# First and last RMS norms of an encoder layer: weight row spread by TensorE, roots by ScalarE and VectorE, last token tile in two halves of its columns

## The chip, the cores and the metric

The kernel runs on one core of a Trainium2 chip. The metric is the device time of one execution in microseconds (us); a kernel's time is the median of its runs. TensorE multiplies matrices, VectorE, ScalarE and GpSimd work elementwise, SyncE issues most of the transfers (DMA); each engine runs its own instructions in the order in which they were compiled and waits for the others by semaphores.

## The reference

One layer of a bidirectional encoder over 1024 tokens of width 1024, all in float32, with 256 memory tokens. Each of three parts is normed ahead and behind and added to the residual stream:

```python
def _rms_norm(x, gain):
    xf = x.astype(jnp.float32)
    y = xf * lax.rsqrt(jnp.mean(xf * xf, axis=-1, keepdims=True) + EPS)
    return (y * gain.astype(jnp.float32)).astype(x.dtype)
...
h = _rms_norm(x, g_mix_pre[l])
proj = h @ w_in[l]
...   # window attention and gated DeltaNet on the columns of proj
x = x + _rms_norm(mix, g_mix_post[l])
...   # cross-attention into the memory
x = x + _rms_norm(c, g_cross_post[l])
f = _swiglu(_rms_norm(x, g_ffn_pre[l]), w_gate_up[l], w_down[l])
x = x + _rms_norm(f, g_ffn_post[l])
```

The change concerns the first of these norms (with `g_mix_pre`, EPS is 1e-6) and the last (with `g_ffn_post`) with the product by `w_down` ahead of it (2816 rows, 1024 columns).

## The kernel before

**Numbers.** TensorE takes a float32 operand as a pair: `split` (L100) has ScalarE round the source to the array's short form (`hi`, the cast in L103) and VectorE or GpSimd subtract it from the source (`lo`, L104). A product is three matmuls, hi by hi, hi by lo, lo by hi, which add up in one PSUM bank of 128 x 512 float32. "Plain" float32 products, with operands that are not split, occur too; the transposes by the identity (`ident`) are of this kind.

**Order.** The program is written with a tile framework. Pools hand out tiles in on-chip memory (SBUF, 128 partitions); a pool stacks its tiles from the low end of memory or, with `side="right"`, from the high end, each tile rounded up to 32 bytes a partition. Tiles of one pool with the same `tag` share `bufs` buffers, so the next one waits until the earlier one has been read. At compile time a scheduler orders each engine's instructions against a timeline of its own; `tc.high_priority(AHEAD)` draws the block's instructions forward in it, and `tc.issue_after(ins)` puts the block's instructions behind `ins` on the engine they share. So the order of the text is not the order of an engine: a change in one place can move instructions elsewhere.

**Memory.** Pool `cst` (L112) holds `ident`, `mhalf` (a constant -0.5) and `cols` at the low end; all pools of the left side, with the weight pool `wp` (L117) first, lie above it. On the right side a filler tile of 32 bytes (`off`, L115) lies ahead of the others.

**The start (L202 to L233).** Six of eight token tiles `xt` (128 tokens x 1024) are loaded at once on SyncE's queue; behind the first come `gmix`, the row `g_mix_pre` repeated for all 128 partitions by the transfer (512 KB), and `ident`. For each tile t: ScalarE squares it into a scrap tile `junk` and sums (`ss`, L221), `rstd_of` (L158) makes the inverse root by two GpSimd instructions (scale and add EPS, L161; power -0.5, L162), VectorE multiplies tile, root and `gmix` (L224), TensorE transposes eight 128 x 128 pieces into two PSUM tiles (L229), and `split` makes `hi` and `lo` of them. Four tiles fill one half (`hT[0]`: `hhi0`, `hlo0`), four the other. Two weight blocks of `w_in` are loaded behind the second and fourth tile (`load_w` in the line of `ws`, `after=xload[t]`) and multiplied by the halves as these get ready (`gemm_b`, L261). What is read from other parameters meanwhile: two mask copies `mU_r`, `mL_r` (L247, L248) on VectorE, three small loads into `prm` (L250 to L252), `nega`, an exponential on ScalarE (L253), and the narrow weight tile `wabr` (L307) on VectorE.

**The middle** (DeltaNet, attention, output projection, cross-attention, gate and up products) is not touched.

**The last product and the end (L1635 to L1768).** The product by `w_down` is made of seven block products of half the tokens by half the columns (11 blocks of 128 rows each); `block_product` makes them for four token tiles at once, into the banks `A`, `D_` and `X` of 128 x 512. The seventh is written out in the loop at L1744: for each of four token tiles t, two strips of the left operand (`atr`, 6 and 5 blocks) are loaded and split, and 33 matmuls add to `X[t]`, which already holds the product before it. The sums that are not `X`'s lie in `za` (columns 512 to 1023 of the output, finished before) and `zv` (columns 0 to 511). Then VectorE adds the bank (L1761), `sq_of` (L1674) has ScalarE square and sum 512 columns into `sq`, VectorE multiplies by the gain row `gp` (which holds the gain times the root of 1024, so that the norm needs a sum and not a mean), `rstd_at` (L1688) makes the root on GpSimd from both halves' sums, and VectorE finishes `za` and `zv` with the root and the residual (`residual`, L1682, loaded again from `d_x2`) and SyncE stores each:

```python
    nc.vector.tensor_tensor(zv[:, t], zv[:, t], X[t], ALU.add)
    sq_of(zv[:, t], r, 0)
    nc.vector.tensor_tensor(zv[:, t], zv[:, t], gp[:, 0:512], ALU.mult)
    rs = rstd_at(r)
    for z, o_ in ((za, 512), (zv, 0)):
        nc.vector.scalar_tensor_tensor(z[:, t], z[:, t], rs, xr[:, o_:o_ + 512], ALU.mult, ALU.add)
        nc.sync.dma_start(out[there(r), o_:o_ + 512], z[:, t])
```

`first_half` (L1723) finishes the other four token tiles, two of them inside this loop. `bank` (L1500) takes a PSUM bank from a pool of eight; four are free by then.

Of the kernel before, what the change touches and what calls it, by code (L numbers as in the profile page):

```python
# [10 lines left out]
F32 = mybir.dt.float32  # L11
F32R = mybir.dt.float32r
I32 = mybir.dt.int32
AF = mybir.ActivationFunctionType
ALU = mybir.AluOpType
# [4 lines left out]
P = 128  # L20
S = 1024
D = 1024
# [4 lines left out]
EPS = 1e-6  # L27
# [49 lines left out]
def tile_hybrid_block(  # L77
# [4 lines left out]
    g_ffn_pre, w_gate_up, w_down, g_ffn_post, consts, out, dump=None, stop=None,  # L82
):
    nc = tc.nc
    x, mem, out = x[0], mem[0], out[0]
# [26 lines left out]
    cst = ctx.enter_context(pool("cst", 1))  # L112
# [20 lines left out]
    ident = cst.tile([P, P], F32, name="ident")  # L133
    mhalf = cst.tile([P, 16], F32, name="mhalf")
    nc.gpsimd.memset(mhalf, -0.5)
    cols = cst.tile([P, P], F32, name="cols")
    p12 = ExitStack()
    sm = p12.enter_context(pool("sm", 1))
# [2 lines left out]
    mU_r = sm.tile([P, P], F32R, name="mU_r")  # L141
    mL_r = sm.tile([P, P], F32R, name="mL_r")
    prm = sm.tile([P, 24], F32, name="prm")
    nega = sm.tile([P, 8], F32, name="nega")
# [10 lines left out]
    cm = {n: (C[:, a - C0:a - C0 + P] if a < C1 else CE[:, a - C1:a - C1 + P]) for n, a in _AT.items() if n != "ident"}  # L155
    rope_f, rope_s = (CE[:, _ROPE_AT - C1 + i:_ROPE_AT - C1 + i + 1] for i in range(2))

    def rstd_of(rs, ss, n, eps):  # L158

        w = ss.shape[-1]  # L160
        nc.gpsimd.tensor_scalar(rs, ss, n, eps, ALU.mult, ALU.add)  # L161
        nc.gpsimd.tensor_tensor(rs, rs, mhalf[:, :w], ALU.pow)  # L162


    gain_at = {"cross": 60, "mem": 60 + KT, "ffn": 60 + 2 * KT}
    r0 = 60 + 3 * KT
# [29 lines left out]
    t1 = pa1.enter_context(pool("t1a", 2, side="right"))  # L196

    def small():
        return ps.tile([P, 512], F32, tag="ps", name="ps")


    xts = [t1.tile([P, D], F32, tag="xt", name="xt", bufs=6) for _ in range(6)]  # L202
    gmix = t1.tile([P, D], F32, tag="gmix", name="gmix", bufs=1)
    xload = []
    for t in range(6):
        xload.append(nc.sync.dma_start(xts[t], x[t * P:(t + 1) * P, :]))
        if t == 0:
            nc.sync.dma_start(gmix, g_mix_pre[0].partition_broadcast(P))
            nc.sync.dma_start(ident, consts[:, 0:P])
    hT = []  # L210
    for hf in range(2):
        hi = hx.tile([P, KT, HALF], F32R, name=f"hhi{hf}")
        lo = hx.tile([P, KT, HALF], F32R, name=f"hlo{hf}")
        for j in range(4):
            t = 4 * hf + j
            xt = xts[t] if t < 6 else t1.tile([P, D], F32, tag="xt", name="xt", bufs=6)
            if t >= 6:
                nc.sync.dma_start(xt, x[t * P:(t + 1) * P, :])
            junk = t1.tile([P, D], F32, tag="junk", name="junk", bufs=1)
            ss = t1.tile([P, 1], F32, tag="ss", name="ss", bufs=4)  # L220
            nc.scalar.activation(junk, xt, AF.Square, accum_out=ss)  # L221
            rs = t1.tile([P, 1], F32, tag="rs", name="rs", bufs=4)
            rstd_of(rs, ss, 1.0 / D, EPS)
            nc.vector.scalar_tensor_tensor(xt, xt, rs, gmix, ALU.mult, ALU.mult)  # L224
            for kq in range(2):
                pt = small()
                for k in range(4):
                    c = (4 * kq + k) * P
                    nc.tensor.transpose(pt[:, k * P:(k + 1) * P], xt[:, c:c + P], ident)  # L229
                o = slice(4 * kq, 4 * kq + 4), slice(j * P, (j + 1) * P)  # L230
                split(hi[:, o[0], o[1]], lo[:, o[0], o[1]], pt.rearrange("p (k t) -> p k t", k=4))
        hT.append((hi, lo))
        dump(f"hT{hf}", (hi, lo))  # L233
# [8 lines left out]
    pt = small()  # L242
# [1 line left out]
    nc.scalar.copy(cols, pt[:, :P])  # L244
    nc.sync.dma_start(CE, consts[:, C1:])
    nc.sync.dma_start(C, consts[:, C0:C1])
    nc.vector.tensor_copy(mU_r, cm["mU"])  # L247
    nc.vector.tensor_copy(mL_r, cm["mL"])  # L248

    nc.sync.dma_start(prm[:, 0:8], a_log[0].rearrange("d h -> (d h)").partition_broadcast(P))  # L250
    nc.sync.dma_start(prm[:, 8:16], dt_bias[0].rearrange("d h -> (d h)").partition_broadcast(P))
    nc.sync.dma_start(prm[:, 16:24], attn_sink[0].partition_broadcast(P))  # L252
    nc.scalar.activation(nega, prm[:, 0:8], AF.Exp)  # L253
    nc.vector.tensor_scalar(nega, nega, -1.0, None, ALU.mult)

    def gemm_b(whi, wlo, act, psums, nk=KT):
# [45 lines left out]
    t1 = pa1.enter_context(pool("t1b", 1, side="right"))  # L302
# [1 line left out]
    wab = t1.tile([P, KT, 16], F32, tag="wab", name="wab", bufs=1)  # L304
    nc.sync.dma_start(wab, w_in[:, 2816:2832].rearrange("(k p) n -> p k n", p=P))
    wabr = tb.tile([P, KT, P], F32R, tag="V", name="wabr", bufs=1)
    nc.vector.tensor_scalar(wabr, hT[0][0].bitcast(F32)[:, :, 0:P], 0.0, None, ALU.mult)  # L307
    nc.vector.tensor_copy(wabr[:, :, 0:16], wab)
    nc.vector.tensor_tensor(wabr[:, :, 16:32], wab, f32(wabr[:, :, 0:16]), ALU.subtract)
    abT = tb.tile([32, S], F32, tag="A", name="abT", bufs=1)  # L310
    for hf in range(2):
        pp = pg.tile([P, 512], F32, tag="pg", name="pg")
        for k in range(KT):
            for a in range(2):
                nc.tensor.matmul(pp, wabr[:, k, :], hT[hf][a][:, k, :], start=(k == 0 and a == 0),
                                 stop=(k == KT - 1 and a == 1))
        nc.scalar.copy(abT[:, hf * HALF:(hf + 1) * HALF], pp[0:32, :])
    pt = small()
# [1180 lines left out]
    def bank(name):  # L1499
        return pg.tile([P, 512], F32, tag="pg", name=name)  # L1500
# [172 lines left out]

    def sq_of(src, t, ch):  # L1674
        jk = tp_.tile([P, 512], F32, tag="jk", name="jk", bufs=1)
        nc.scalar.activation(jk, src, AF.Square, accum_out=sq[:, ch, t:t + 1])  # L1676

    def there(t):
        r = (t + NT // 2) % NT
        return slice(r * P, (r + 1) * P)  # L1680
# [7 lines left out]
    def rstd_at(t):  # L1688

        rs = tp_.tile([P, 1], F32, tag="frs", name="frs")  # L1690
        nc.gpsimd.tensor_scalar(rs, sq[:, 1, t:t + 1], sq[:, 0, t:t + 1], D * EPS, ALU.add, ALU.add)  # L1691
        nc.gpsimd.tensor_tensor(rs, rs, mhalf[:, 0:1], ALU.pow)
        return rs
# [46 lines left out]
    for t in range(4):  # L1740
        nc.vector.tensor_tensor(za[:, t], za[:, t], X[t], ALU.add)
        sq_of(za[:, t], 4 + t, 1)

    for t in range(4):  # L1744
        tt = slice(t * P, (t + 1) * P)
        for k0, n in ((0, 6), (6, 5)):
            with tc.high_priority(AHEAD):
                ar = wp.tile([P, KT, P], F32, tag="wraw", name="atr")[:, 0:n]
                nc.sync.dma_start(ar, d_a["22"][k0:k0 + n, :, tt].rearrange("f p n -> p f n"))
                ah, al = [wp.tile([P, KT, P], F32R, tag=g, name=g)[:, 0:n] for g in ("whi", "wlo")]  # L1750
                split(ah, al, ar)
            for k in range(n):
                for i, (a, w) in enumerate(((ah, t4h), (ah, t4l), (al, t4h))):
                    nc.tensor.matmul(X[t], a[:, k], w[:, k0 + k], start=False, stop=(k0 + k == NB - 1 and i == 2),  # L1754
                                     skip_group_check=True)
        if t < 2:
            first_half(2 + t)
        r = 4 + t
        xr = residual(r)
        nc.vector.tensor_tensor(za[:, t], za[:, t], gp[:, 512:], ALU.mult)  # L1760
        nc.vector.tensor_tensor(zv[:, t], zv[:, t], X[t], ALU.add)  # L1761
        sq_of(zv[:, t], r, 0)
        nc.vector.tensor_tensor(zv[:, t], zv[:, t], gp[:, 0:512], ALU.mult)
        rs = rstd_at(r)
        for z, o_ in ((za, 512), (zv, 0)):
            nc.vector.scalar_tensor_tensor(z[:, t], z[:, t], rs, xr[:, o_:o_ + 512], ALU.mult, ALU.add)
            nc.sync.dma_start(out[there(r), o_:o_ + 512], z[:, t])
    LB.close()  # L1768
    L0.close()

# [29 lines left out]
```

## Time and profile before

| | us |
|---|---|
| median of three runs | 1534.2 |
| lowest and highest | 1531.57, 1537.82 |
| the profiled execution | 1537.92 |
| its span, from first to last instruction or transfer | 1536.2 |
| TensorE busy, 0 to 30 / 30 to 1500 / 1500 to 1528.3 / behind it | 16.89 / 1431.81 / 28.28 / 0.00 |

The profiled execution ran at a granted TensorE clock of 0.992 (1 is full speed). In the profile, an operation is named by engine and line: PE is a matmul on TensorE, PEld the load of its stationary operand, DVE VectorE, ACT ScalarE, POOL GpSimd, SP SyncE; a "q" behind it is the engine's sequencer, which waits and issues. `ps<-ident,xt` is a tile and what it is made from; `x16` counts the instructions that a row takes together; what stands in brackets is the idle time ahead of it and what ended it. A matmul's own duration overlaps with the next one's, so a row of n matmuls is read by its whole length. In a window's row each engine has its busy time and number of instructions, in the order PE, PEld, DVE, ACT, POOL; then the granted clock and the transfers. In a row of a group, the numbers behind the bar are busy us of all, mean ns of one, and idle us of the engine ahead of them.

### The profile page before, as it was taken

To read this page: it belongs to the slowest core of one execution; us is meant where nothing else is said; L and a number is where in the kernel's file an instruction comes from. 1 tells how busy PE (TensorE), PEld (TensorE's weight loads), DVE (VectorE), ACT (ScalarE), POOL (GpSimd) and SP (SyncE) were. 2 spreads that over 40 slices of the span, in tenths; PEclk is the share of its full clock that TensorE was granted. 3 is DMA by queue.
4 is the path that set the end of the run, shared out by engine and by line. 5 is a ranking of instruction groups with operands and counts; after the bars stand their busy time and mean duration, and the time that the engine had idled before them with its cause. 6 is when DMAs were issued, how large, how long until landed. Compare 5 with 4: busy or idle time off the path is not lost.

```text
span 1536.2 us, 21190 instructions
## 1 busy us (share of the span) xinstructions
PE 1477.0 (96%) x7403; PEld 1241.1 (81%) x7403; DVE 1109.5 (72%) x1790; ACT 742.3 (48%) x1516; POOL 396.3 (26%) x404
## 2 busy tenths in 40 slices
PE   6999999999999999999999898999999999999997
PEld 5888878878899778887888686888888888888786
DVE  6868999787888865538466876676877555696665
ACT  5678821447557764456454663323223332454532
POOL 2020221311326203242201622343443332000021
PEclk9999999999999999999999999999999999999999
DMA  6235575856987684457725534343533333863354
GB/s 207 76 105 151 144 194 152 218 161 181 317 285 233 196 284 155 152 160 261 236 89 185 192 129 125 124 131 110 172 123 102 104 103 103 317 214 95 106 176 166
DMA packets 272360, 258.70 MB, mean 168 GB/s; under 512 B 34793, under 2 KB 204670, under 8 KB 272254
## 3 DMA queue, kind: packets, MB, share of 16 engines
q1 hardware_dynamic: 272253, 257.35, 53.3%
q8 instruction: 58, 0.95, 0.3%
q14 instruction: 49, 0.39, 0.1%
HBM read 179.41 MB, written 75.27 MB: 166 GB/s over the span
## 4 chain that ended last, share of the span: by engine, by line
PE 70%; DVE 11%; DMA 8%; ACT 6%; issue 3%; SPq 1%; POOL 1%; DVEq 0%; POOLq 0%; ACTq 0%
PE pE L1466 8%; PE pD L1466 8%; PE pA L1466 7%; PE pg L261 6%; PE pmg L1070 6%; PE pdX L1657 6%; PE pcq L261 4%; PE pdA L1657 4%; PE pB L1466 4%; PE pst L1286 3%; PE psc L809 2%; PE pdX L1754 2%; PE pdD L1657 2%; DVE acc L286 2%; DMA wraw<-in_w_ckv_dram 1%
## 5 line engine op out<-in xcount | busy, mean ns | idle before, releaser
L103 ACT CAST whi<-wraw 128x1024 fp32r<-128x1024 f32 x96 | 100.9, 1052 | 142.6 <-DMA wraw<-in_w_gate_up_dram 29.5
L104 POOL TENSOR_TENSOR wlo<-wraw,whi 128x1024 fp32r<-128x1024 f32 x38 | 91.9, 2419 | 188.9 <-ACT whi L103 180.2
L261 PE MATMUL pg<-hlo,whi 128*128 128x512 f32 x352 | 139.5, 397 | 0.0
L261 PE MATMUL pg<-hhi,whi 128*128 128x512 f32 x352 | 139.2, 396 | 0.0
L261 PE MATMUL pg<-hhi,wlo 128*128 128x512 f32 x352 | 138.4, 394 | 0.0
L1466 PE MATMUL pA<-b,whi 128*128 128x512 f32 x352 | 113.1, 402 | 5.9 <-ACT m L1483 3.4
L104 DVE TENSOR_TENSOR wlo<-wraw,whi 128x1024 fp32r<-128x1024 f32 x58 | 73.7, 1272 | 42.2 <-ACT whi L103 39.7
L1466 PEld LDWEIGHTS pA<-b,whi 128*128 128x128 f32 x352 | 67.4, 193 | 20.3 <-ACT m L1483 3.8
L1657 PE MATMUL pdX<-dhl,whi 128*128 128x512 f32 x264 | 76.1, 391 | 1.5 <-ACT dhl L103 0.8
L261 PEld LDWEIGHTS pg<-hhi,whi 128*128 128x128 f32 x352 | 66.5, 189 | 13.3 <-ACT hhi L103 0.2
L261 PEld LDWEIGHTS pg<-hhi,wlo 128*128 128x128 f32 x352 | 66.5, 189 | 12.8
L261 PEld LDWEIGHTS pg<-hlo,whi 128*128 128x128 f32 x352 | 66.4, 189 | 12.7
L1544 POOL TENSOR_TENSOR act<-act,up 128x512 f32<-128x512 f32 x33 | 49.5, 1501 | 95.9 <-DVE up L1543 62.6
L1466 PE MATMUL pA<-b,wlo 128*128 128x512 f32 x176 | 69.9, 398 | 0.0
L103 ACT CAST whi<-araw 128x1024 fp32r<-128x1024 f32 (+1 forms) x36 | 35.3, 981 | 67.7 <-PE pdX L1657 24.4
L104 DVE TENSOR_TENSOR wlo<-araw,whi 128x1024 fp32r<-128x1024 f32 (+1 forms) x36 | 40.8, 1134 | 35.0 <-ACT whi L103 34.9
L1516 POOL TENSOR_TENSOR sr<-wraw 128x512 f32<-128x512 f32 x22 | 30.0, 1366 | 130.4 <-DMA wraw<-in_w_gate_up_dram 119.1
L286 DVE SCALAR_TENSOR_TENSOR acc<-cp,cols,acc 128x1024 f32<-128x1024 f32 x48 | 62.1, 1295 | 0.1
L1691 POOL TENSOR_SCALAR frs<-sq 128x1 f32<-128x1 f32 x8 | 11.9, 1496 | 193.6 <-ACT jk L1676 192.7
L1657 PEld LDWEIGHTS pdX<-dhl,whi 128*128 128x128 f32 x264 | 49.3, 188 | 12.8 <-ACT dhl L103 1.1
L1466 PE MATMUL pB<-s0h,s1h 128*128 128x512 f32 x176 | 54.4, 391 | 3.4 <-ACT s1h L103 3.4
L103 ACT CAST dhl<-b 128x512 fp32r<-128x512 f32 x66 | 40.3, 620 | 31.6 <-PE pdA L1657 13.7
(481 smaller groups left out, 4302.2 us busy)
## 6 DMA issues: line engine op xcount, KB each, us to landing
wraw<-in_w_gate_up_dram SPq DMA_DIRECT2D x52, 512.0 KB, 3.9
kv<-d_kv SPq DMA_DIRECT2D x32, 512.0 KB, 6.8
wraw<-in_w_in_dram SPq DMA_DIRECT2D x22, 512.0 KB, 4.2
b<-in_w_down_dram SPq DMA_DIRECT2D x20, 512.0 KB, 7.7
araw<-d_as SPq DMA_DIRECT2D x20, 512.0 KB, 3.7
pz<-d_pz SPq DMA_DIRECT2D x32, 256.0 KB, 7.3
wraw<-in_w_ckv_dram SPq DMA_DIRECT2D x16, 512.0 KB, 5.1
wraw<-in_w_out_dram SPq DMA_DIRECT2D x16, 512.0 KB, 3.7
```

The source lines that it names most:

```text
L103: nc.scalar.copy(hi, src)
L104: (eng or nc.vector).tensor_tensor(lo, src, f32(hi), ALU.subtract)
L261: nc.tensor.matmul(p_, w[:, k, :], ah[a][:, k, :], start=(k == 0 and i == 0), stop=(k == nk - 1 and i == 2))
L286: nc.vector.scalar_tensor_tensor(acc, cp[:, t:t + S], taps[t], acc, ALU.mult, ALU.add)
L809: nc.tensor.matmul(out[:, d, h, :], lt[:, d, h, :], rt[:, d, h, :], start=True, stop=True)
L1070: nc.tensor.matmul(pp[t], act[a][:, k, tt], w_[:, kk, :], start=(k == 0 and i == 0), stop=(k == KT - 1 and i == 2))
L1286: nc.tensor.matmul(bank, a[:, tt], w, start=(start and i == 0), stop=(stop and i == 2), skip_group_check=not check)
L1466: nc.tensor.matmul(out_, w[a][:, k, :], xx[b_][:, k, :], start=(start and k == 0 and i == 0), stop=(k == HK - 1 and i == 2), skip_group_ch ...
L1516: nc.gpsimd.tensor_tensor(s[0], b_[:, 0:HK], b_[:, HK:], ALU.add)
L1544: nc.gpsimd.tensor_tensor(o_, o_, up, ALU.mult)
L1657: nc.tensor.matmul(banks[t], a[:, k - k0, tt], w, start=(first and k == 0 and i == 0), stop=(k == NB - 1 and i == 2), skip_group_check=not ...
L1754: nc.tensor.matmul(X[t], a[:, k], w[:, k0 + k], start=False, stop=(k0 + k == NB - 1 and i == 2), skip_group_check=True)
```

## The change

At the start, `gmix` is no longer spread by the transfer. A single row `grow` (4 KB) is loaded ahead of all, and two plain float32 matmuls against a row of ones, `one`, write it to 128 partitions of two PSUM tiles, from which VectorE copies it. `grow` has the tag of `junk`, which has one buffer. The inverse roots are ScalarE's square root (with scale, and EPS from a tile `epsc`) and VectorE's reciprocal (`inverse_root`) in place of two GpSimd instructions; a root of EPS (`warm`) is made ahead of them. `mU_r`, `mL_r` and `wabr` are ordered behind the last tile's scaling on VectorE and `nega` behind its root on ScalarE.

At the end, the fourth token tile's 33 matmuls of 512 columns become 33 of columns 0 to 255, into the bank it had, and 33 of columns 256 to 511, into a new bank `XL`, to which nothing was added before; the earlier content of that half of `X[3]` is added to `zv` ahead of the loop. Sum, square and gain are done for each half, `known` collects EPS and the sums on VectorE, the root is made by `inverse_root`, in all four tiles, and the fourth tile's `zv` is finished and stored in two halves. The strips' two inner loops become one list, `tiles`.

```diff
@@ constants
+    epsc = cst.tile([P, 1], F32, name="epsc")
+    nc.gpsimd.memset(epsc, EPS)
@@ behind rstd_of
+    def inverse_root(rs, ss, scale, bias):
+        root = nc.scalar.activation(rs, ss, AF.Sqrt, bias=bias, scale=scale)
+        nc.vector.reciprocal(rs, rs)
+        return root
@@ the start
+    grow = t1.tile([1, D], F32, tag="junk", name="grow", bufs=1)
+    one = cst.tile([1, P], F32, name="one")
+    nc.gpsimd.memset(one, 1.0)
     xload = []
     for t in range(6):
+        if t == 0:
+            nc.sync.dma_start(grow, g_mix_pre)
         xload.append(nc.sync.dma_start(xts[t], x[t * P:(t + 1) * P, :]))
         if t == 0:
-            nc.sync.dma_start(gmix, g_mix_pre[0].partition_broadcast(P))
             nc.sync.dma_start(ident, consts[:, 0:P])
+    warm = t1.tile([P, 1], F32, tag="ss", name="warm", bufs=4)
+    nc.scalar.activation(warm, epsc, AF.Sqrt)
+    for ch in range(2):
+        pt = small()
+        nc.tensor.matmul(pt, one, grow[:, ch * 512:(ch + 1) * 512], start=True, stop=True)
+        nc.vector.tensor_copy(gmix[:, ch * 512:(ch + 1) * 512], pt)
...
-            rstd_of(rs, ss, 1.0 / D, EPS)
-            nc.vector.scalar_tensor_tensor(xt, xt, rs, gmix, ALU.mult, ALU.mult)
+            rooted = inverse_root(rs, ss, 1.0 / D, epsc)
+            scaled = nc.vector.scalar_tensor_tensor(xt, xt, rs, gmix, ALU.mult, ALU.mult)
...
-    nc.vector.tensor_copy(mU_r, cm["mU"])
-    nc.vector.tensor_copy(mL_r, cm["mL"])
+    with tc.issue_after(scaled.ins):
+        nc.vector.tensor_copy(mU_r, cm["mU"])
+        nc.vector.tensor_copy(mL_r, cm["mL"])
...
-    nc.scalar.activation(nega, prm[:, 0:8], AF.Exp)
+    with tc.issue_after(rooted.ins):
+        nc.scalar.activation(nega, prm[:, 0:8], AF.Exp)
...
-    nc.vector.tensor_scalar(wabr, hT[0][0].bitcast(F32)[:, :, 0:P], 0.0, None, ALU.mult)
+    with tc.issue_after(scaled.ins):
+        nc.vector.tensor_scalar(wabr, hT[0][0].bitcast(F32)[:, :, 0:P], 0.0, None, ALU.mult)
@@ sq_of
-        nc.scalar.activation(jk, src, AF.Square, accum_out=sq[:, ch, t:t + 1])
+        nc.scalar.activation(jk[:, 0:src.shape[-1]], src, AF.Square, accum_out=sq[:, ch, t:t + 1])
@@ the end
+    nc.vector.tensor_tensor(zv[:, 3, 256:], zv[:, 3, 256:], X[3][:, 256:], ALU.add)
+    XL = bank("pdY")
 
     for t in range(4):
         tt = slice(t * P, (t + 1) * P)
+        tiles = []
...
-            for k in range(n):
+            tiles += [(ah[:, k], al[:, k]) for k in range(n)]
+        columns = [(slice(0, 512), X[t])] if t < 3 else [(slice(0, 256), X[t][:, 0:256]), (slice(256, 512), XL[:, 0:256])]
+        for c_, p_ in columns:
+            fresh = c_.start > 0
+            for k, (ah, al) in enumerate(tiles):
                 for i, (a, w) in enumerate(((ah, t4h), (ah, t4l), (al, t4h))):
-                    nc.tensor.matmul(X[t], a[:, k], w[:, k0 + k], start=False, stop=(k0 + k == NB - 1 and i == 2),
-                                     skip_group_check=True)
+                    nc.tensor.matmul(p_, a, w[:, k, c_], start=(fresh and k == 0 and i == 0), stop=(k == NB - 1 and i == 2),
+                                     skip_group_check=not fresh)
...
-        nc.vector.tensor_tensor(zv[:, t], zv[:, t], X[t], ALU.add)
-        sq_of(zv[:, t], r, 0)
-        nc.vector.tensor_tensor(zv[:, t], zv[:, t], gp[:, 0:512], ALU.mult)
-        rs = rstd_at(r)
-        for z, o_ in ((za, 512), (zv, 0)):
-            nc.vector.scalar_tensor_tensor(z[:, t], z[:, t], rs, xr[:, o_:o_ + 512], ALU.mult, ALU.add)
-            nc.sync.dma_start(out[there(r), o_:o_ + 512], z[:, t])
+        known = sq[:, 1, r:r + 1]
+        nc.vector.tensor_scalar(known, known, D * EPS, None, ALU.add)
+        for c_, p_ in columns:
+            nc.vector.tensor_tensor(zv[:, t, c_], zv[:, t, c_], p_, ALU.add)
+            sq_of(zv[:, t, c_], r, 0)
+            nc.vector.tensor_tensor(zv[:, t, c_], zv[:, t, c_], gp[:, c_], ALU.mult)
+            if c_.stop < 512:
+                nc.vector.tensor_tensor(known, known, sq[:, 0, r:r + 1], ALU.add)
+        rs = tp_.tile([P, 1], F32, tag="frs", name="frs")
+        inverse_root(rs, sq[:, 0, r:r + 1], 1.0, known)
+        for z, o_, c_ in [(za, 512, slice(0, 512))] + [(zv, 0, c_) for c_, _ in columns]:
+            at = slice(o_ + c_.start, o_ + c_.stop)
+            nc.vector.scalar_tensor_tensor(z[:, t, c_], z[:, t, c_], rs, xr[:, at], ALU.mult, ALU.add)
+            nc.sync.dma_start(out[there(r), at], z[:, t, c_])
```

## The prediction

> **What bounds the kernel now.** I read the page first, then the chain of waits, then the timeline at both ends of the span. The page gives busy time and share of each engine, TensorE's busy tenths in 40 slices, and the chain that ended last by engine.
>
> ```profile
> PE 1477.0 (96%) x7403; PEld 1241.1 (81%) x7403; DVE 1109.5 (72%) x1790; ACT 742.3 (48%) x1516; POOL 396.3 (26%) x404
> PE   6999999999999999999999898999999999999997
> PE 70%; DVE 11%; DMA 8%; ACT 6%; issue 3%; SPq 1%; POOL 1%; DVEq 0%; POOLq 0%; ACTq 0%
> ```
>
> TensorE bounds everything but the first slice and the last, and those are what the change touches. What shortens the start moves all later products forward; what shortens the tail ends the span. First TensorE's timeline at the start (start, us, operation, [idle before]):
>
> ```profile
> 16.26 4.03 PE L229 MATMUL ps<-ident,xt 128*128 128x128 f32 x16 [2.32 <-DVE xt L224]
> 20.11 1.22 PE L261 MATMUL pg<-hhi,whi 128*128 128x512 f32 x2
> 21.88 4.01 PE L229 MATMUL ps<-ident,xt 128*128 128x128 f32 x16 [0.54 <-DVE xt L224]
> 25.54 0.63 PE L261 MATMUL pg<-hlo,whi 128*128 128x512 f32 x1
> ...
> 32.17 1.03 PE L229 MATMUL ps<-ident,xt 128*128 128x128 f32 x8
> ```
>
> From 25.54 TensorE never stops; six tiles are transposed before it, at about 0.25 us a piece, against 0.13 at 32.17: the array is on half pace until then. The same stretch on the other engines, a window of it (its last two numbers are the share of the DMA queues and GB/s), and two loads:
>
> ```profile
> 4.46 1.06 ACT L221 ACTIVATE junk<-xt 128x1024 f32<-128x1024 f32 x1 [2.40 <-DMA xt<-in_x_dram]
> 8.53 1.06 ACT L221 ACTIVATE junk<-xt 128x1024 f32<-128x1024 f32 x1 [2.92 <-DMA xt<-in_x_dram]
> ...
> 14.97 1.28 POOL L161 TENSOR_SCALAR rs<-ss 128x1 f32<-128x1 f32 x1
> 16.34 0.55 POOL L162 TENSOR_TENSOR rs<-rs,mhalf 128x1 f32<-128x1 f32 x1
> 16.92 1.28 DVE L224 SCALAR_TENSOR_TENSOR xt<-xt,rs,gmix 128x1024 f32<-128x1024 f32 x1
> ...
> 20.33 0.59 ACT L103 CAST hhi<-ps 128x512 fp32r<-128x512 f32 x1 [0.27 <-PE ps L229]
> ...
> 22.69 1.06 ACT L221 ACTIVATE junk<-xt 128x1024 f32<-128x1024 f32 x1 [1.77 <-DMA xt<-in_x_dram]
> ```
>
> ```profile
> 12.00:16.00 4.00, 1.94 (x8) 1.54 (x8) 3.93 (x5) 3.86 (x8) 3.01 (x3) 1.00 1.09 358
> ```
>
> ```profile
> gmix<-in_g_mix_pre_dram SPq DMA_DIRECT2D x1, 512.0 KB, 5.0
> ...
> wab<-in_w_in_dram SPq DMA_DIRECT2D x1, 64.0 KB, 2.1
> ```
>
> ScalarE waits for x, the queues are full, and the 512 KB of the spread row lie ahead of the second tile. GpSimd's two steps to a root take 1.28 and 0.55 us here, and VectorE's scaling follows them. The chain at the end, then the timeline's rows behind it:
>
> ```profile
> 1499.91 28.39 PE pdX L1754 x125
> ...
> 1528.32 0.70 DVE zv L1761
> ...
> 1529.10 0.63 ACT jk L1676
> ...
> 1529.92 0.80 POOL frs L1691
> ...
> 1531.39 0.75 DVE za L1766
> ```
>
> ```profile
> 1529.64 0.19 ACT L1676 ACTIVATION_READ_ACCUMULATOR jk<-zv 128x1 f32 x1
> 1529.86 0.69 DVE L1763 TENSOR_TENSOR zv<-zv,gpost 128x512 f32<-128x512 f32 x1 [0.85 <-ACT jk L1676]
> ...
> 1532.06 0.75 DVE L1766 SCALAR_TENSOR_TENSOR zv<-zv,frs,xrf 128x512 f32<-128x512 f32 x1
> 1532.17 0.33 SPq L1767 DMA_DIRECT2D out_dram<-za  x1
> 1532.84 0.33 SPq L1767 DMA_DIRECT2D out_dram<-zv  x1
> ```
>
> From the first read of the last bank to the last store's issue is 1532.84 - 1528.32 = 4.52 us, one operation at a time; the store takes the remaining 3.4 to 1536.2.
>
> **The tail.** Rows for the small and halved operations, and two of nine products of 256 columns that follow each other:
>
> ```profile
> L886 DVE TENSOR_TENSOR ol<-ol,of 128x256 f32<-128x256 f32 x4 | 1.5, 414 | 0.0
> L669 DVE RECIPROCAL es<-es 128x4 f32<-128x4 f32 x16 | 2.8, 172 | 0.3
> L667 ACT ACTIVATE es<-es 128x4 f32<-128x4 f32 x16 | 3.2, 198 | 10.9 <-POOL es L666 10.9
> L1487 ACT ACT_TABLE_LOAD x1 | 1.3, 1283 | 0.0
> ```
>
> ```profile
> 387.44 0.29 PE L949 MATMUL pck<-mT,wlo 128*128 128x256 f32 x1
> ...
> 388.51 0.28 PE L949 MATMUL pck<-mT,wlo 128*128 128x256 f32 x1
> ```
>
> Ten products start from 387.44 to 388.51, so one each 0.119 us; 125 of 512 columns in 28.39 are 0.227 each. The last tile's 33 products become 66: 66 x 0.119 - 33 x 0.227 = +0.36. In the compiled order TensorE mixes the two halves; the left one is complete 19 products, 2.3 us, ahead of the end. Its work (add 0.41, square with its read-out 0.52, gain 0.41, sum 0.2) is 1.6 and hides there. For the right half, from the bank's completion: add 0.41, hand-over 0.08, square 0.52 to its sum (0.73 from 1529.10 to 1529.83, less 0.21: 512 columns more cost 0.43, from 0.63 to 1.06), then the product by the gain, which waits for the square as at 1529.86 and goes ahead of the reciprocal on VectorE: 0.40, under which ScalarE's root of 0.28 (198 ns, plus an estimated 0.08 for a second operand) hides; reciprocal 0.17, za 0.67 (start to start), the halves of zv 0.40 and 0.48 (1.28 for 1024 columns, 0.75 for 512, so 0.48 for 256), issue 0.03. Sum 3.16, against 4.52: -1.36. Were the halves nearly as dear as whole operations, another 0.7 would come back; were the short ones to overlap more, 0.4 more would go. The last store carries half the bytes, but three leave in place of two: 0, between -0.4 and +0.3.
>
> The root needs another table, loaded once, in the first of the four last tiles. Behind it on ScalarE stands a cast:
>
> ```profile
> 1509.74 0.84 ACT L103 CAST whi<-atr 128x768 fp32r<-128x768 f32 x1 [2.39 <-PE pdX L1754]
> ```
>
> Load and root are 1.28 + 0.28 = 1.56, inside the 2.39 for which ScalarE waits for TensorE anyway: 0. Without that cover it would still be a cast made 3 us ahead of its product. The extra add of the right half and four small sums (0.41 + 0.2 each) stand on VectorE in TensorE's shadow: 0.
>
> **The start.** Removed: the 512 KB load, which lets tiles two to six come about 1.5 us earlier (512 KB at 358 GB/s), and GpSimd's roots. Added: two fp32 products of 512 columns from one row, two copies, a root and a reciprocal a tile, one table load (ahead of x) and one behind the last root. The row's tile shares its buffer with the squares' scrap tile, so the first square waits for both products. The nearest row of a plain fp32 product:
>
> ```profile
> 107.61 1.95 PE L458 MATMUL ps<-acc 128*128 128x128 f32 x16
> ```
>
> Two records make one product there, (1.95 - 0.27) / 15 = 0.112 each, so 128 columns cost 0.22, 512 cost 0.9, and 1.8 on half pace. The 4 KB row lands some 2.1 us after its issue at 0.8 (by the 64 KB row above): the first square starts at 2.9 + 2 x 1.8 + 0.2 = 6.7, not 4.46; on full pace at 4.9. Then ScalarE waits for no load. Ahead of the fourth tile's scaling VectorE now has the second tile's remainders, which follow five squares (5 x 1.06), four casts (4 x 0.55), two weight blocks (2 x 1.0) and four roots (4 x 0.25) on ScalarE: 6.7 + 10.5, remainder 0.7, scaling 1.3: transposes at 19.2, where before they began at 18.2 (16.92 + 1.28). They, the two products and 16 more transposes take 2.0 + 1.0 + 4.0 on half pace: products go on at 26.2, not 25.54: +0.6. But TensorE is now busy without a break from 19.2; if it gets full pace before the fifth tile (22.2), 2 of these 4 us go: 24.2, or -1.3; with a first square at 4.9 as well, -2. I take -0.4, the middle of +0.6 and -1.3, since the rows show five busy microseconds without the change of pace (16.26 to 21.3) and then the change near 25.9.
>
> [...]
>
> What is moved: SP now issues the seventh tile's load behind three small parameter loads and a weight block, and ScalarE has the fourth tile's last cast behind that tile's square. TensorE needs that cast some 13 products (2.9 us) after 26.2; 1.7 us for square and cast leave until 27.4 for the load, which before was there at 22.6. Cost 0, +1 for each us past that.
>
> Sum: -1.36 + 0.36 - 0.4 = -1.4. The profiled execution took 1537.92 around its span of 1536.2, 3.7 above the median: 1536.5 for it, **1532.8** for the median of 1534.2.
>
> **Rivals.** *The grid shift, slower.* epsc and one lie low in memory, and all tiles above start 544 bytes higher. In the compiled kernel before, each tile that TensorE or a transfer of size touches starts at a multiple of 64 bytes; after, an operand of 5129 of 6944 TensorE instructions and 69% of the bytes transferred start 32 past one. No row has that for either. The nearest is VectorE reading cp at odd offsets, against an aligned one:
>
> ```profile
> L286 DVE SCALAR_TENSOR_TENSOR acc<-cp,cols,acc 128x1024 f32<-128x1024 f32 x48 | 62.1, 1295 | 0.1
> L224 DVE SCALAR_TENSOR_TENSOR xt<-xt,rs,gmix 128x1024 f32<-128x1024 f32 x8 | 10.2, 1280 | 9.5 <-POOL rs L162 9.3
> ```
>
> 1.2% more, on 74% of 1477 us, is +13: 1545.9; no cost is the other end, and what I take, since 1.2% may be the odd offset alone. It decides from +9 (a product of 0.227 at 0.229). Transfers could carry it too where they are near full:
>
> ```profile
> 360.00:420.00 60.00, 53.87 (x403) 49.62 (x402) 50.87 (x134) 37.46 (x83) 15.71 (x15) 1.00 0.95 288
> ```
>
> [...]
>
> *Weight loads pace the halves*, by their own length:
>
> ```profile
> L1466 PEld LDWEIGHTS pA<-b,whi 128*128 128x128 f32 x352 | 67.4, 193 | 20.3 <-ACT m L1483 3.8
> ```
>
> 0.19 in place of 0.119 adds 4.7: 1537.5. Against it, the nine intervals above, with a load each. *The start stalls* behind the seventh tile's load, 3 us: 1535.8. For it, the full queues; against it, that 512 KB less precede it. *Full pace comes in time*, -2 for the start: 1531.2. *The mixed order undoes the halving*, the left half's 1.6 back on the path: 1534.4; against it, 2.3 us of cover.
>
> **How the numbers follow.** Forecast 0.46, grid shift 0.24, weight loads 0.05, stall 0.07, full pace 0.12, mixed order 0.06. The forecast's own range is 1529 to 1537: start -2 to +0.6, tail (bounds above, store and products with it) -1.8 to 0, and medians of three that spread by 3. The range, 1528.5 to 1546, takes in the grid shift's price and leaves 0.05 below and 0.13 above. About 0.5%, 7.7 us, can be told from no change: faster than 1526.5 takes more than both ends have, 0.05; slower than 1541.9 is most of the grid shift and a longer stall, 0.22; within, 0.73.
>
> **What would show it.** Right: 66 products 0.119 apart at the end, 3.2 us from the last bank's first read to the last issue, first square near 6.7, unbroken products from about 26. Wrong: intervals of 512-column products off 0.227 or longer landings (grid), idle time of TensorE on ACT before its 15th product (stall), or a gap in the middle that today's trace lacks, for which I have no price.

## The result, and the profile after

| | before | changed |
|---|---|---|
| median of 7 runs each, us | 1532.93 | 1544.73 |
| lowest to highest | 1530.78 to 1538.32 | 1539.44 to 1546.05 |
| profiled execution / its span | 1537.92 / 1536.2 | 1544.21 / 1542.5 |

The changed kernel is slower: its time is 1.0057 times that before, with an interval of 1.0039 to 1.0074, where the forecast was 1.4 us less. Busy times on the page of the changed kernel, against the first line of the prediction:

```profile
PE 1494.1 (97%) x7440; PEld 1242.8 (81%) x7440; DVE 1112.9 (72%) x1813; ACT 748.0 (48%) x1533; POOL 381.6 (25%) x382
```

TensorE works 17.1 us longer for nearly the same work. To see where, one looks for a stretch in which it never waits, and counts. Two windows of the changed kernel, in the gate and up stage and in the last product (behind the range in us its length, then busy time and number of instructions of TensorE, its weight loads, VectorE, ScalarE and GpSimd; the last three are granted clock, DMA share and GB/s):

```profile
960.00:1130.00 170.00, 170.00 (x735) 137.52 (x734) 122.65 (x147) 48.65 (x81) 65.21 (x41) 1.00 0.40 127
1330.00:1490.00 160.00, 158.51 (x698) 130.44 (x697) 119.07 (x170) 77.55 (x123) 8.69 (x5) 1.00 0.49 171
```

The same windows of the kernel before:

```profile
960.00:1130.00 170.00, 170.00 (x752) 140.84 (x751) 125.07 (x150) 50.21 (x83) 64.66 (x41) 1.00 0.40 127
1330.00:1490.00 160.00, 158.50 (x697) 130.28 (x696) 117.58 (x166) 75.67 (x120) 10.55 (x6) 1.00 0.50 168
```

With TensorE busy throughout and the clock at 1.00 in both, 735 products go through where 752 went before; in the later stage nothing has changed. The timeline splits the first stage by kind of product. These rows begin blocks of 12 products, before:

```profile
970.84 0.61 PE L1466 MATMUL pB<-s0h,s1h 128*128 128x512 f32 x2
...
973.55 0.62 PE L1466 MATMUL pD<-b,s0h 128*128 128x512 f32 x2
...
976.27 0.61 PE L1466 MATMUL pE<-b,s2h 128*128 128x512 f32 x2
...
978.99 0.62 PE L1466 MATMUL pA<-b,whi 128*128 128x512 f32 x2
...
981.71 0.62 PE L1466 MATMUL pB<-s0h,s1h 128*128 128x512 f32 x2
```

and in the changed kernel:

```profile
970.29 0.63 PE L1486 MATMUL pB<-s0h,s1h 128*128 128x512 f32 x2
...
973.04 0.63 PE L1486 MATMUL pD<-b,s0h 128*128 128x512 f32 x2
...
975.84 0.63 PE L1486 MATMUL pE<-b,s2h 128*128 128x512 f32 x2
...
978.64 0.62 PE L1486 MATMUL pA<-b,whi 128*128 128x512 f32 x2
...
981.40 0.63 PE L1486 MATMUL pB<-s0h,s1h 128*128 128x512 f32 x2
```

Before, every block takes 2.72 us (0.227 a product). Changed, pB takes 2.75 and pA 2.76, but pD and pE take 2.80 (0.233). What sets these apart is where their operands lie: pB has both on the right side of memory, pA both on the left, pD and pE the moving one (named first) on the left and the stationary one (which a weight load, PEld, brings in) on the right. The left side rose by 544 bytes, the right side stayed. That pB and pA lose 0.03 to 0.04 us a block too, this does not explain.

At the start, TensorE's timeline of the changed kernel (rows where it waits or slows), and then ScalarE's and SP's:

```profile
2.30 3.75 PE L225 MATMUL ps<-grow,one 1*128 1x512 f32 x4 [2.30 <-POOL dmask L436]
...
24.71 0.48 PE L280 MATMUL pg<-hlo,whi 128*128 128x512 f32 x1
...
29.53 0.50 PE L280 MATMUL pg<-hhi,whi 128*128 128x512 f32 x1 [2.02 <-ACT hhi L103]
...
30.63 0.63 PE L280 MATMUL pg<-hlo,whi 128*128 128x512 f32 x1
31.06 0.63 PE L280 MATMUL pg<-hhi,wlo 128*128 128x512 f32 x1
```

```profile
6.09 1.06 ACT L238 ACTIVATE junk<-xt 128x1024 f32<-128x1024 f32 x1 [3.80 <-PE ps L225]
...
27.86 1.06 ACT L238 ACTIVATE junk<-xt 128x1024 f32<-128x1024 f32 x1 [6.61 <-DMA xt<-in_x_dram]
...
28.91 0.57 ACT L103 CAST hhi<-ps 128x512 fp32r<-128x512 f32 x1
```

```profile
18.21 0.38 SPq L126 DMA_DIRECT2D wraw<-in_w_in_dram  x1
18.69 3.52 SPq L235 DMA_DIRECT2D xt<-in_x_dram  x2
```

Products go on at 24.71, 0.8 us sooner than before. But the seventh tile's load, issued behind a weight block, is there only at 27.86 (22.69 before), the fourth tile's last cast stands behind its square, and TensorE waits 2.02 us for that cast. About 1 us later the products come 0.43 us apart, and a window shows the granted clock at half:

```profile
30.60:33.60 3.00, 3.00 (x8) 2.32 (x7) 2.38 (x3) 2.98 (x7) 0.00 (x0) 0.50 0.00 0
```

At the end, VectorE's and SP's rows from the last bank's first read:

```profile
1536.29 0.42 DVE L1791 TENSOR_TENSOR zv<-zv,pdY 128x256 f32<-128x256 f32 x1 [0.78 <-PE pdY L1781]
1537.35 0.42 DVE L1793 TENSOR_TENSOR zv<-zv,gpost 128x256 f32<-128x256 f32 x1 [0.64 <-ACT jk L1696]
1537.69 0.15 DVE L169 RECIPROCAL frs<-frs 128x1 f32<-128x1 f32 x1
1537.88 0.75 DVE L1800 SCALAR_TENSOR_TENSOR za<-za,frs,xrf 128x512 f32<-128x512 f32 x1
1538.55 0.88 DVE L1800 SCALAR_TENSOR_TENSOR zv<-zv,frs,xrf 128x256 f32<-128x256 f32 x2
```

```profile
1539.09 0.88 SPq L1801 DMA_DIRECT2D out_dram<-zv  x2
```

The second half is ready at 1538.55 + 0.88 = 1539.43, 3.1 us behind the first read; the span ends 6.2 us behind it, where before it ended 7.9 behind (1536.2 - 1528.32).

### The profile page after: what moved, and what is told of

Its sections match the earlier page's. It is cut to its first block, busy times and chain, and to the rows that moved or that the text cites. A ratio compares the mean times of both kernels' runs of the same rounds, so it can differ in the third digit from the quotient of the medians.

```text
span 1542.5 us, 21281 instructions
## 1 busy us (share of the span) xinstructions
PE 1494.1 (97%) x7440; PEld 1242.8 (81%) x7440; DVE 1112.9 (72%) x1813; ACT 748.0 (48%) x1533; POOL 381.6 (25%) x382
## 4 chain that ended last, share of the span: by engine, by line
PE 71%; DVE 10%; DMA 8%; ACT 5%; issue 3%; SPq 2%; POOL 1%; DVEq 0%; ACTq 0%; POOLq 0%
PE pD L1486 8%; PE pE L1486 8%; PE pA L1486 7%; PE pg L280 6%; PE pmg L1090 6%; PE pdX L1677 6%; PE pcq L280 4%; PE pB L1486 4%; PE pdA L1677 4%; PE pst L1306 3%; PE psc L829 2%; PE pdD L1677 2%; PE pco L1205 1%; PE pdX L1781 1%; DMA xt<-in_x_dram 1%
## 5 line engine op out<-in xcount | busy, mean ns | idle before, releaser
L1486 PE MATMUL pD<-b,s0h 128*128 128x512 f32 x176 | 56.7, 403 | 0.0
L1537 DVE TENSOR_TENSOR sr<-sr,wraw 128x512 f32<-128x512 f32 x22 | 37.3, 1694 | 26.5 <-POOL sr L1536 26.5
```

Source lines behind the costliest of these rows:

```text
L1486: nc.tensor.matmul(out_, w[a][:, k, :], xx[b_][:, k, :], start=(start and k == 0 and i == 0), stop=(k == HK - 1 and i == 2), skip_group_ch ...
L1537: nc.vector.tensor_tensor(s[1], s[0], a_[:, 0:HK], ALU.subtract)
```

## The experiments

All ratios are to the kernel before on the same chip. "Distance" is what the experiments vary: by how much the left side rose plus by how much the right side dropped, against the kernel before, modulo 256; in the compiled kernel before, both operands of 6165 of its 6909 products start at 192 modulo 256, and 5180 of its 5276 products of 512 columns have operands a multiple of 256 apart; the other 96 are 128 apart. "Stage" is the gate and up stage, and "own pool" means `epsc` and `one` in a pool that closes after the start. Products are counted in the window from 960 to 1130; the stage runs from the first product of pB to the first of pdA.

| kernel | left up | right down | distance | products | stage, us | ratio (95%) |
|---|---|---|---|---|---|---|
| before | 0 | 0 | 0 | 752 | 377.5 | 1 |
| changed | 544 | 0 | 32 | 735 | 385.8 | 1.0057 (1.0039 to 1.0074) |
| e1 changed, 64-byte epsc | 576 | 0 | 64 | 741 | 382.2 | 1.0008 (0.9994 to 1.0021) |
| e2 before, left 32 | 32 | 0 | 32 | 734 | 386.5 | 1.0095 (1.0076 to 1.0114) |
| e3 changed, both 32 | 544 | 32 | 64 | 741 | 382.7 | 1.0046 (1.0029 to 1.0064) |
| e4 before, right 32 | 0 | 32 | 32 | 735 | 386.3 | 1.0070 (1.0051 to 1.0088) |
| e5 changed, own pool | 0 | 0 | 0 | 752 | 377.6 | 0.9989 (0.9974 to 1.0003) |
| e6 before, both | 224 | 32 | 0 | 751 | 377.9 | 0.9999 (0.9982 to 1.0015) |
| e7 before, left 128 | 128 | 0 | 128 | 737 | 384.7 | 1.0061 (1.0039 to 1.0082) |
| e8 before again | 0 | 0 | 0 | 751 | 377.7 | one run, 1531.21 us |
| e9 end alone | 0 | 0 | 0 | 752 | 378.0 | 0.9998 (0.9984 to 1.0011) |
| e10 start alone | 0 | 0 | 0 | 751 | 377.6 | 0.9998 (0.9988 to 1.0009) |
| e11 seven buffers | 0 | 0 | 0 | 752 | 377.1 | 1.0098 (1.0081 to 1.0116) |
| e12b ScalarE's queue | 0 | 0 | 0 | 752 | 377.2 | 0.9998 (0.9984 to 1.0012) |

**The changed kernel back on the 64-byte grid.**

```diff
-    epsc = cst.tile([P, 1], F32, name="epsc")
+    epsc = cst.tile([P, 16], F32, name="epsc")[:, 0:1]
```

> The changed kernel with epsc 64 bytes wide, so that the left side starts 576 bytes higher in place of 544 and all operands of TensorE begin at multiples of 64 bytes again; the order on every engine is that of the changed kernel. Grid (the shift of 32 bytes costs): the gate and up stage has 0.2267 us a product again, not 0.227 to 0.234, and takes 8 us less; ratio to before 0.998 to 1.001, by the start's stall (+0 to +2 that is left of it later) and the tail's -1. Schedule (start and tail themselves cost the 8 us): as the changed kernel, 1.0057, same pace as it.

The time came out as the grid theory has it, but the pace did not: 741 products, not 752. Its blocks of 12, by the timeline:

```profile
977.01 0.62 PE L1486 MATMUL pB<-s0h,s1h 128*128 128x512 f32 x2
...
979.74 0.63 PE L1486 MATMUL pD<-b,s0h 128*128 128x512 f32 x2
...
982.50 0.62 PE L1486 MATMUL pE<-b,s2h 128*128 128x512 f32 x2
...
985.26 0.62 PE L1486 MATMUL pA<-b,whi 128*128 128x512 f32 x2
...
987.99 0.62 PE L1486 MATMUL pD<-x,s3h 128*128 128x512 f32 x2
...
990.74 0.63 PE L1486 MATMUL pE<-s0l,bhi 128*128 128x512 f32 x2
...
993.54 0.62 PE L1486 MATMUL pA<-b,whi 128*128 128x512 f32 x2
```

pA and pB take 2.73, pD and the first pE 2.75 to 2.76, and the pE of s0l by bhi, whose moving operand is on the right and whose stationary one is on the left, 2.80. All start at multiples of 64 bytes, so a grid of 64 is not what counts; and the sign matters: with the moving operand 64 above the stationary one a product costs 0.003 us more, with it 64 below 0.007.

**The shift alone, on either side, without the change.**

```diff
-    mhalf = cst.tile([P, 16], F32, name="mhalf")
+    mhalf = cst.tile([P, 24], F32, name="mhalf")
```

> The kernel before with mhalf 32 bytes wider: nothing else moves, every left-side tile above it starts 32 bytes off the 64-byte grid, the right side does not. Grid: 512-column products whose moving and stationary operands lie 32 bytes apart modulo 64 (2720 of 5276) take 0.234, the others 0.227; 8 us slower, ratio 1.005. Schedule: ratio 1.000.

```diff
-    nc.gpsimd.memset(off.tile([P, 8], F32, name="off"), 0.0)
+    nc.gpsimd.memset(off.tile([P, 16], F32, name="off"), 0.0)
```

> The kernel before with the right side's filler doubled: only the right side is 32 off. Relative: the same 2720 products are out of step as with the wider mhalf, same ratio 1.005, the same groups at 0.234. Absolute by the moving operand: 1736 + 264 products slow, those between two right-side tiles (pB, both off) among them, and the ones with a left-side moving tile (pD, pE of b by s) not.

Thirty-two bytes of unused memory make the kernel before slower by 0.95% on one side and by 0.70% on the other, 14.6 and 10.7 us, both more than the 1.005 expected, with 734 and 735 products: what the changed kernel has in this stage, with neither its start nor its end. With the right side moved, the blocks start so:

```profile
973.21 0.63 PE L1466 MATMUL pB<-s0h,s1h 128*128 128x512 f32 x2
...
975.95 0.63 PE L1466 MATMUL pD<-b,s0h 128*128 128x512 f32 x2
...
978.75 0.63 PE L1466 MATMUL pE<-b,s2h 128*128 128x512 f32 x2
```

pD, whose moving operand stayed, takes 2.80; pB, both of whose operands moved, 2.74. That pD and pE are slow whichever side moved speaks for the pair and against the moving operand alone.

**Both sides off, and a distance of 128.** The changed kernel with the right side's filler doubled:

> The changed kernel with the right side's filler doubled to 64 bytes: now both sides are 32 off the grid, and moving and stationary operand of all 512-column products are in step again. Relative (the pair counts, not each operand by itself): as with the 64-byte epsc, 0.2267 throughout, ratio 0.998 to 1.001. Absolute (an operand or a transfer off the grid costs by itself): slower than the changed kernel, all 5245 products at 0.234, ratio 1.008 or more. Transfers (the landings carry it): no faster than the changed kernel either.

Neither theory as written: 741 products and 1.0046. The right side grows downwards, so 544 up and 32 down make 576, and the pace is that of the 64-byte epsc, whose sides stand 576 apart too, though there every operand was on the grid and here none. That suggested the distance, with a period above 64.

The times of these two kernels differ more than their pace: 1.0008 and 1.0046, with intervals that do not meet, at stages of 382.2 and 382.7 us. They differ in one thing more. On the left side, where 61% of the bytes transferred to or from on-chip memory start, e1 has them at a multiple of 256 and e3 at 224 modulo 256; and in a stretch in which transfers are near full, e1 and then e3 show

```profile
360.00:420.00 60.00, 56.42 (x420) 51.75 (x419) 51.83 (x134) 39.94 (x91) 17.30 (x16) 1.00 0.93 299
```

```profile
360.00:420.00 60.00, 54.27 (x389) 48.97 (x388) 49.50 (x131) 40.86 (x89) 16.19 (x16) 1.00 0.96 282
```

The 299 GB/s are the most of all traces in this stretch. Whether faster transfers are why e1 loses less than its pace would cost was not tried; it stays open.

The distance was then tried with the kernel before and both sides moved (mhalf 72 columns wide, off 16):

> The kernel before with the left side 224 bytes higher and the right side 32 lower: every operand is 32 off the 64-byte grid, but moving and stationary are 256 apart from where they were. Distance with a period of 256 or less: ratio 1.000, 752 products. Absolute (each operand or transfer off the grid costs): ratio 1.005 to 1.010, 735 or fewer. A period above 256 would give the same slowing, which the pace of pairs within one side (pA, pB) tells apart: they stay at 0.2267 then.

```profile
960.00:1130.00 170.00, 170.00 (x751) 140.77 (x751) 123.65 (x149) 50.36 (x83) 64.12 (x41) 1.00 0.40 127
```

Both operands of every product of 512 columns are 32 bytes off the grid, the sides are 256 further apart, and nothing is lost. So neither an operand off 64 bytes nor a transfer off it has a cost that shows here; 256 apart is as good as 0. With mhalf 48 columns wide:

> The kernel before with the left side 128 bytes higher, on the 64-byte grid. Distance with a period of 64 or 128: 752 products, ratio 1.000 (a period of 64 is already unlikely by the 741 of the 64-byte epsc). With a period of 256: slower, ratio 1.002 to 1.008. Absolute: ratio 1.000.

```profile
960.00:1130.00 170.00, 170.00 (x737) 138.00 (x736) 124.46 (x148) 49.06 (x82) 66.71 (x43) 1.00 0.38 121
```

A multiple of 64, and slow: pD and pE take 2.79 to 2.80 here, so the period is not 128 or less. If the pace repeats with the distance, it does so every 256 bytes. The kernel before bears this out in its own trace. Its operands are 256 or 768 apart modulo 1024 in 2936 of its products of 512 columns and 0 or 512 in 2244, and in the gate and up stage both kinds come 0.227 us apart. And twelve of the 96 products that are 128 apart run from the first of these rows to the second:

```profile
823.84 0.40 PE L1185 MATMUL pco<-cph,vr 128*128 128x512 f32 x1
...
826.63 0.63 PE L1286 MATMUL pst<-wpart,b 128*128 128x512 f32 x2
```

That is 2.79 us, as in e7, in a kernel to which nothing was done.

**The change without the shift.** epsc and one are temporary; in the start's own pool they move nothing that lasts:

```diff
-    epsc = cst.tile([P, 1], F32, name="epsc")
-    one = cst.tile([1, P], F32, name="one")
+    one = t1.tile([1, P], F32, name="one", bufs=1)
+    epsc = t1.tile([P, 1], F32, name="epsc", bufs=1)
```

> The changed kernel with epsc and one in the start's own pool on the right, which is closed later: all lasting tiles have exactly the addresses they had before, the order on every engine stays that of the changed kernel. Distance (the pace hangs on moving minus stationary address, modulo more than 64; the 576 of the 64-byte epsc left 64): 0.2267 in the gate and up stage, 752 products between 960 and 1130 as before, not 741; faster than the changed kernel by 8 to 12 us, ratio 0.996 to 0.9995. Chip (the 0.2267 was that of another chip): 735 to 741 products again, ratio 1.001 as with the 64-byte epsc.

```profile
960.00:1130.00 170.00, 170.00 (x752) 140.73 (x751) 122.00 (x146) 50.38 (x83) 63.36 (x41) 1.00 0.40 129
```

The pace of before is back to the product. The ratio is 0.9989, 1.6 us less than before, with an interval that still reaches 1.0003; against the changed kernel it is 1.0057 / 0.9989, or 0.68%, 10.4 us (some 3.5 either way by the two intervals; the two ratios are from different chips). This is the fastest of all kernels here by its ratio, but it isn't shown to beat the kernel before. The kernel before, unchanged, traced again on this chip:

> The kernel before unchanged, for a second trace on the chip of these runs. Distance: 752 products between 960 and 1130, and a time near the 1533 to 1536 of its runs, so some 2 to 4 us less than its first profile, somewhere outside that stage. Chip: 741 or fewer.

751 products, so it was not the chip; and this execution's span, 1529.5, is 6.7 shorter than the first trace's (2 to 4 were expected), nearly all of it gained between 49 and 933 us.

**The end alone, the start alone.** Each kernel takes one part, end or start, from the version with the own pool and the rest from the kernel before.

> The kernel before with the changed end alone (halves, sums, root); every address and the order of everything ahead of the last loop stay those of before. Own working of the prediction: 3.2 us from the first read of the last bank to the last issue, in place of 4.52, 0.36 us more of products: ratio 0.9993. Halving undone by the mixed order: 1.000. 752 products between 960 and 1130.

> The kernel before with the changed start alone, epsc and one in the start's own pool, so that all lasting addresses are those of before. Stall (the seventh tile's load comes behind the third weight block): the transpose of the parameter rows, at 33.5 to 34.6 in the traces of the start before, comes at 35 to 38.5, and TensorE waits 0.7 to 2 us for the fourth tile's last cast; ratio 1.000 to 1.002. Start faster, as priced in the prediction: 0.4 us less, ratio 0.9997.

Both ratios are 0.9998: nothing that can be told from no change. In the traces the end is worth what it should be: from the first product by `t4h` (the seventh block's part of `w_down`) to the end of the span, the seven traces with the old end take 38.0 to 38.6 us, the seven with the new one 36.9 to 37.6, 1.1 less on average. The start alone waits as in the changed kernel; its rows on TensorE and ScalarE:

```profile
28.50 0.50 PE L280 MATMUL pg<-hhi,whi 128*128 128x512 f32 x1 [1.63 <-ACT hhi L103]
```

```profile
26.82 1.06 ACT L238 ACTIVATE junk<-xt 128x1024 f32<-128x1024 f32 x1 [5.82 <-DMA xt<-in_x_dram]
```

and its first product by `wabr` comes at 49.81, where four traces with the old start and distance 0 have 47.9 to 49.0. That microsecond doesn't show at the end.

**The seventh load earlier.** First by a seventh buffer (`bufs=7`, the load in the first loop), then by issuing it from ScalarE:

```diff
-                nc.sync.dma_start(xt, x[t * P:(t + 1) * P, :])
+                (nc.scalar if t == 6 else nc.sync).dma_start(xt, x[t * P:(t + 1) * P, :])
```

> The changed kernel with epsc and one in the start's pool and a seventh buffer for the token tiles, so that the seventh load is issued at once behind the sixth, ahead of the parameters and the third weight block (the scheduler orders some of the middle anew). Stall: no wait of TensorE for the fourth tile's cast, the transpose of the parameter rows at 33 to 34; 2 to 4 us less than without the seventh buffer, ratio to before 0.9965 to 0.998. Rival (what the start loses is made up by 366 us, as the traces of before with 4 us between them show): ratio 0.999 as without it.

TensorE no longer waits for the cast, but the start gains next to nothing: the first product by `wabr` comes at 50.05, in e5 at 50.35; TensorE had waited 0.94 us for an earlier cast, and its products came 0.43 us apart up to 27.4. And the kernel is 1% slower. The scheduler had ordered the middle anew, and there it lost 13.9 us against e5 by the first product of pB: a window of the middle, of this kernel and then of the kernel before again,

```profile
220.00:320.00 100.00, 94.02 (x491) 79.90 (x490) 77.35 (x161) 26.34 (x59) 27.54 (x46) 0.95 0.70 180
```

```profile
220.00:320.00 100.00, 97.20 (x537) 82.42 (x535) 83.96 (x183) 32.91 (x79) 28.41 (x48) 1.00 0.72 180
```

46 products fewer in 100 us, with TensorE idle for 6 us of them and its granted clock at 0.95. Which of the moved instructions does it was not tried.

> The changed kernel with epsc and one in the start's pool, and the seventh tile's load issued by ScalarE behind the third tile's first cast, not by SP behind the third weight block; every other instruction stands where it stood with them in that pool. Stall: the load lands by 22, TensorE does not wait for the fourth tile's last cast, nor does its clock fall behind it; the transpose of the parameter rows at 33 to 34.5, not at 36.8; at the end 1 to 3 us less, ratio 0.997 to 0.9985. Rival (later waits make up for the start): the same at 34 us, but a ratio of 0.999, as without it.

The wait is gone, and a new one came. ScalarE's and TensorE's rows:

```profile
16.27 0.38 ACTq L235 DMA_DIRECT2D xt<-in_x_dram  x1
16.69 1.05 ACT L103 CAST whi<-wraw 128x1024 fp32r<-128x1024 f32 x1 [2.45 <-DMA CE<-in_consts_dram]
```

```profile
22.10 1.94 PE L246 MATMUL ps<-ident,xt 128*128 128x128 f32 x8 [4.78 <-DVE rs L167]
```

ScalarE stood 2.45 us at this issue, and what is behind it came later, so that the fourth tile's transposes started at 22.10 and not at 19.8. The first product by `wabr` came at 51.62, and the transpose of the parameter rows at 38.1, not at the 33 to 34.5 expected. And the profiled execution still was the shortest of all, 1528.8: 3.7 us late against the second trace of before at 49 us, 1.2 at 933, level at 1491. That is one execution; the ratio is 0.9998, so at the end nothing shows, which is the rival of this experiment, though the start it assumed did not come.

## Why the prediction was wrong

**The step that failed** is in the rivals: "no cost is the other end, and what I take, since 1.2% may be the odd offset alone". The grid shift was named, its products were counted and its price put at +13 us with a chance of 0.24; it is what happened, and the runs with and without it (e5 against the changed kernel) put it at 10.4 us. Taking nothing for a cost that spans 74% of TensorE's time, on no row for it, decided the forecast. A row was there: the twelve pco products of the kernel before, 2.79 us where twelve others take 2.72.

**The mechanism under its name was also wrong.** The prediction asked whether an operand lies off a multiple of 64 bytes. In e6 both operands of all products of 512 columns do, at no cost; in e1 and e7 none does, at a cost. What the runs follow is the distance of moving and stationary operand: 734 to 741 products in the window at 32, 64 and 128, 751 or 752 at 0 and 256. The 5129 instructions are about those whose stationary operand moved off the grid (by the compiled kernel 5131; with either operand 6119), and neither count is that distance. So the row with VectorE at odd offsets was no neighbour of the question, and 13 came near 10.4 by luck: of the changed kernel's 5245 products of 512 columns 2722 were out of step by the shift, at 0.006 to 0.007 us each some 17 us of TensorE's time; its busy time is 17.1 above before and 14.0 above e5, which differs by the addresses. 10.4 us of it show at the end. In the traces of e5 and the changed kernel, also 10.4 apart, 8.2 arise in the gate and up stage, where TensorE next to never waits, and 2.0 are there by the first product by `wabr`, where of the two only the changed kernel had the half clock. That transfers start 32 off a multiple of 64 had no part that shows: in e6 all of size did, and its interval is 2.8 us down to 2.3 us up.

**The start.** Mis-sized: -0.4 was taken. Two products of 1.8 us each and a first square at 6.7 were forecast; the four records take 3.75 us and the square came at 6.09. Products went on at 24.71, inside 24.2 to 26.2, because the granted clock, 0.51 from 21.5 to 23.7, was 1.00 from there to 25.5, and 16 transposes of the fifth and sixth tiles took 2.55 us and not 4.0. The change of pace near 25.9, on which the -0.4 leaned, is no fixed point. Between 12 and 21 us of e5 TensorE had only these:

```profile
13.56 3.96 PE L246 MATMUL ps<-ident,xt 128*128 128x128 f32 x16 [2.40 <-DVE xt L241]
19.84 1.07 PE L246 MATMUL ps<-ident,xt 128*128 128x128 f32 x8 [2.31 <-DVE rs L167]
```

The first sixteen run at 0.25 us each, the eight after them at 0.13; in e3, behind sixteen in 3.96 us as well, the eight took 1.94, or 0.24 each. What sets the moment of the change, no trace shows.

But "cost 0, +1 for each us past that", for the seventh tile's load, had the wrong deadline: 27.4 was counted from products at 26.2; counted from 24.71 it is 25.9, the load came at 27.86, and the wait was 2.02. The half clock behind it cost 8 products 0.2 each, 1.6 more. That is the rival "the start stalls", priced at 3 us with 0.07. At the first product by `wabr` the changed starts of e5 and e10 are some 1.6 us late on average, but e10 shows none of it at the end within its 0.1%.

**The end.** Right: 3.16 us from first read to last issue were forecast, and 3.1 to the last result measured. The 0.08 for a second operand in ScalarE's root was a guess that no row showed; the root took 0.29 (at 1537.35), where 0.28 was assumed, and lay under the product by the gain. The products of the halves start 0.11 and 0.13 us apart in turn, and five of seven traces wait 0.2 to 0.3 us for a remainder of the second strip, so that on average the bank is complete 0.6 later, not 0.36; from its first read to the end of the span it is 1.7 less, where 1.36 was forecast and the last store put at 0. Net 1.1 less in the traces, against 1.0.

**The sum for what the change does** was -1.4, and with the addresses held (e5) it is -1.6 (between -4.0 and +0.5). That agrees, but is not told from nothing, and the start by itself came out late, not early. What is shown is that the kernel is slower because of 544 bytes.

## What to carry to other kernels

A new constant at the bottom of a stacked memory is a change to every product above it (here 544 bytes, and 10.4 us): put what is temporary into a pool that closes, and look in the compiled kernel at the start addresses of moving and stationary operands, modulo 256, before and after. To find such a cost, count products in a window where TensorE is never idle (here 735 against 752 in 170 us); it needs no model and no quiet chip. And a scheduler that orders a whole program anew can take back more than an edit at its start is worth (e11, 1% slower), so compare the order too.

## What the hardware showed that was not expected

In the gate and up stage a product of 512 columns took 0.2267 us in the kernel before, whose moving and stationary operands start there at the same address modulo 256, and up to 0.2335 in the changed kernel, where those of pD and pE do not, at the same clock of 1.00 and with TensorE never idle. By block of 12: 32 apart in either direction 2.80 us, 64 up 2.76, 64 down 2.80, 128 apart 2.79 to 2.80, 256 apart 2.72. In kernels with such products the blocks at distance 0 take 2.73 to 2.76 as well. Why, no trace shows.

A wait of 2.02 us was followed, 1 us after work went on, by 3 us at a granted clock of 0.50; waits of 1.30 (e5), 1.38 (e3) and 1.63 (e10) at the same place are followed by a clock of 1.00 up to 36 us, and behind 0.68 (e1) the products come 0.23 us apart. What halves the clock, no trace shows.

Executions of one kernel differ by several us in the middle: the two traces of before are 1.2 us apart at 49 us, 7.8 at the first pB (938.76 and 930.93), and 6.7 at the end.
